# The four token-side sums of the block products: issued inside the first gate chunk, and their transposes spread over the first up chunk

## The chip, the cores and the metric

The kernel runs on one core of a Trainium2 chip. The metric is the device time of one execution in microseconds (us); a kernel is timed in several runs, and the median counts. One execution of each kernel is also profiled: its trace holds every instruction of TensorE (PE, its weight loads apart as PEld), VectorE (DVE), ScalarE (ACT), GpSimd (POOL) and SyncE (SP, which issues most of the transfers), all in us from the start of the span.

## The reference

The program is a two-layer encoder trunk over 256 tokens of width 2048. Each layer has a projection into two groups of heads (attention and retention), an output projection with a residual LayerNorm, and a SwiGLU feed-forward part with another. The change touches the feed-forward part alone:

```
for l in range(DEPTH):                       # DEPTH = 2
    ...                                      # heads, w_out
    x = layer_norm(ALPHA * x + mix, ln1_g[l], ln1_b[l])
    f = (jax.nn.silu(x @ w_gate[l]) * (x @ w_up[l])) @ w_down[l]
    x = layer_norm(ALPHA * x + f, ln2_g[l], ln2_b[l])
```

Here `w_gate` and `w_up` are 2048 x 5632 and `w_down` is 5632 x 2048, all in fp32.

## The kernel before, in words

**Precision by splitting.** Each fp32 operand is split in two parts: `hi`, a rounded copy made by ACT, and `lo`, the rest, made by DVE (`split`, the lines 248 and 249). A product is then three matmuls: hi with hi, hi with lo, lo with hi (`mm_x`, the lines 236 to 238). Weights come in units of at most 128 x 2048 elements (four blocks of 128 rows by 512 columns). Unit by unit they are loaded into a `raw` buffer, split into `hi` and `lo` (three buffers of each), used and given back; `W.done()` marks a unit as used and issues the split of the unit three further on, and loads ahead of that. The split of unit n+3 writes the buffer of unit n, so ACT's cast waits until PE has used unit n up.

**Feed-forward part.** The 5632 columns go in chunks of 512. In each layer chunk 0 is computed plainly (`plain_group`): gate chunk, 4 units; two SiLU evaluations; up chunk, 4 units. The two groups of 128 tokens have a PSUM bank each (`gb0`, `gb1` for the gate, `ub0`, `ub1` for the up chunk). A unit is 12 matmuls of 512 columns for each of the two. The other ten chunks are computed as block products with seven multiplications in place of eight (`strassen_group`). These need four sums of the 128 x 512 quarters of `x`, which don't depend on the chunk: `s_forms` makes them once a layer, in `plain_group`. It issues four sums on DVE (the lines 745 to 748, tiles `sf`), turns each by four transposes on PE into a bank (line 752, tile `pts`, 16 transposes of 128 x 128 in all), and splits each turned sum (tiles `sfh`, `sfl`). The first sum is first used in the third unit of chunk 1.

**What surrounds it.** `x` reaches the gate chunk through the LayerNorm of the attention part. `chunk_head` computes the gate chunk while the norm is still being applied: eight pieces (`norm.apply`: two DVE instructions in place on `res`, the lines 275 and 276, four transposes into a bank `ptx`, a split into `xTh` and `xTl`) are taken off the list `pend` by `pop` between the units. It holds three units at a time, uses them for the first 128 tokens, then for the others, and ends with the fourth unit. By the end of `pop(8)` all eight pieces have been issued, so `res` is final from there on.

**What sets the order.** The code is issued through a tile framework whose scheduler places each instruction in the queue of its engine, mostly in the order of the code. Every engine then works through its queue strictly in that order; an instruction that waits for a semaphore holds up what stands behind it on the engine.

Of the kernel before, what the change touches and what calls it, by code (L numbers as in the profile page):

```python
# [18 lines left out]
P = 128  # L19
# [91 lines left out]
def trunk(ctx: ExitStack, tc: tile.TileContext, x, pos, w, lnp, cols, eye, consts, out):  # L111
    nc = tc.nc
    V, A, PE, G = nc.vector, nc.scalar, nc.tensor, nc.gpsimd
# [8 lines left out]
    xTh = const.tile([P, KD, S], F32R, name="xTh")  # L122
    xTl = const.tile([P, KD, S], F32R, name="xTl")
# [7 lines left out]
    ident = const.tile([P, P], F32, name="ident")  # L131

    def bank(tag_name):
        return psp.tile([P, 512], F32, tag="ps", name=tag_name)
# [96 lines left out]
    def mm_x(ps, ncol, tok, unit, xh, xl, k0, nk, first, last):  # L231
        wh, wl = unit
        for k in range(nk):
            sh = xh[:, k0 + k, tok * P:(tok + 1) * P]
            sl = xl[:, k0 + k, tok * P:(tok + 1) * P]
            PE.matmul(ps[:, :ncol], sh, wh[:, k, :ncol], start=first and k == 0, stop=False)  # L236
            PE.matmul(ps[:, :ncol], sh, wl[:, k, :ncol], start=False, stop=False)  # L237
            PE.matmul(ps[:, :ncol], sl, wh[:, k, :ncol], start=False, stop=last and k == nk - 1)  # L238
# [8 lines left out]
    def split(hi, lo, src):  # L247
        A.copy(hi, src)  # L248
        V.tensor_tensor(lo, src, hi.bitcast(F32), ALU.subtract)  # L249
# [36 lines left out]
    def pop(n=1):  # L286
        for _ in range(n):
            if pend:
                pend.pop(0)()

    def chunk_plain(banks, ncol, nu, xh, xl, k0, first=True, last=True):
        for u in range(nu):
            (unit,) = W.get()
            for tok in range(2):
                mm_x(banks[tok], ncol, tok, unit, xh, xl, k0 + 4 * u, 4, first and u == 0, last and u == nu - 1)
            W.done()

    def chunk_head(banks, ncol, nu, xh, xl):
        units = W.get(3)
        for u in range(3):  # L300
            mm_x(banks[0], ncol, 0, units[u], xh, xl, 4 * u, 4, u == 0, False)
            pop(1)
        pop(1)
        for u in range(3):
            mm_x(banks[1], ncol, 1, units[u], xh, xl, 4 * u, 4, u == 0, False)
            W.done()
            pop(1)
        pop(8)
        for u in range(3, nu):
            (unit,) = W.get()  # L310
            for tok in range(2):
                mm_x(banks[tok], ncol, tok, unit, xh, xl, 4 * u, 4, False, u == nu - 1)
            W.done()
# [55 lines left out]
    first = W.start()  # L369
# [45 lines left out]
    for l in range(DEPTH):  # L415
# [9 lines left out]

        cq = [bank(f"cq{t}") for t in range(2)]
        chunk_head(cq, 512, 4, xTh, xTl)
        if l == 0:
            rope_tables()
        ckv = [bank(f"ckv{t}") for t in range(2)]  # L430
        chunk_plain(ckv, 320, 4, xTh, xTl, 0)

        cqTh = att.tile([P, 4, S], F32R, tag="s1", name="cqTh")
# [117 lines left out]
        for t in range(2):  # L551
            pt = bank("pqr")
# [162 lines left out]
        mixh, mixl = Mix(mixAh, mixRh), Mix(mixAl, mixRl)  # L715
        wb = [bank(f"wo2{t}") for t in range(2)]
        chunk_plain(wb, 512, 4, mixh, mixl, 0)
        for t in range(2):
            resid(wb, 2, t, norm)
# [19 lines left out]
        def vt512(name):  # L739
            return ffp.tile([P, 512], F32, tag="v", bufs=8, name=name)  # L740

        def s_forms():
            x_ = lambda t, c: res[:, t, 512 * c:512 * (c + 1)]
            s1, s2, s3, s4 = (vt512(f"sf{i}") for i in range(4))
            V.tensor_tensor(s1, x_(1, 0), x_(1, 1), ALU.subtract)
            V.tensor_tensor(s2, x_(0, 0), s1, ALU.subtract)
            V.tensor_tensor(s3, x_(1, 0), x_(0, 0), ALU.subtract)
            V.tensor_tensor(s4, x_(0, 1), s2, ALU.subtract)
            for i, t in enumerate((s1, s2, s3, s4)):
                pt = bank("pts")  # L750
                for j in range(4):
                    PE.transpose(pt[:, j * P:(j + 1) * P], t[:, j * P:(j + 1) * P], ident)
                split(sfh[:, i, :, :], sfl[:, i, :, :], pt.rearrange("p (j t) -> p j t", j=4))

        hprev = []
# [10 lines left out]

        def plain_group(c, flush):
            gb = [bank(f"gb{t}") for t in range(2)]
            chunk_head(gb, 512, 4, xTh, xTl)
            sg = []  # L770
            for t in range(2):
                s_ = vt512("sg")
                A.activation(s_, gb[t], AF.Silu)
                sg.append(s_)
            flush()
            s_forms()
            ub = [bank(f"ub{t}") for t in range(2)]
            chunk_plain(ub, 512, 4, xTh, xTl, 0)
            for t in range(2):
                V.tensor_tensor(sg[t], sg[t], ub[t], ALU.mult)  # L780
                hprev.append((t, c, sg[t]))
# [79 lines left out]
        for f0, f1 in FF_PARTS:  # L861
# [4 lines left out]
            for c in range(f0, f1):  # L866
                (strassen_group if c else plain_group)(c, flush)
            first, final = f0 == 0, f1 == NFF
            if final:
                g, b = ln_params(ffp, ("sfh", "sfl"), 2 + 2 * l)  # L870
            nu = f1 - f0
            for n in range(4):
# [11 lines left out]
                else:  # L884
                    last = l == DEPTH - 1
# [114 lines left out]
```

## Time and profile before

| | before |
|---|---|
| runs | 2242.03, 2242.4 and 2243.55 us, median 2242.4 us |
| profiled execution | 2244.02 us; its span, first to last instruction, 2242.2 us |
| PE busy | 2200.6 us, 98% of the span |
| DVE busy | 1591.3 us, 71% |
| ACT busy | 1026.0 us, 46% |
| POOL busy | 35.5 us, 2% |
| moved by DMA | 441.22 MB, 197 GB/s on the mean |
| mean granted TensorE clock | 0.995 of full speed |

Busy is the time in which an engine has at least one instruction under way. Matmuls overlap: one of 512 columns lasts some 0.40 us in the trace, but in an undisturbed stream one begins every 0.233 us. [...]

### The profile page before, as it was taken

How to read it: one execution, taken by the hardware profiler on the slowest of the kernel's cores; microseconds unless marked ns; L12 is line 12 of the kernel's file. 1: busy time of each engine (PE TensorE's matmuls, PEld its weight loads, DVE VectorE, ACT ScalarE, POOL GpSimd, SP SyncE). 2: the span in 40 equal slices, each digit the busy share in tenths (PEclk: the TensorE clock that was granted, in tenths of full speed). 3: DMA queues.
4: the chain of work that ended last, by engine and by line, in shares of the span. 5: the costliest groups of instructions: out<-in, count | busy, mean ns of one | idle time of the engine just before them, and what ended most of it. 6: DMA issues, size and time to landing. Idle time of an engine off the chain costs nothing. (4 is left out here: it accounts for less than half of the span.)

```text
span 2242.2 us, 26855 instructions
## 1 busy us (share of the span) xinstructions
PE 2200.6 (98%) x11084; PEld 1846.4 (82%) x11084; DVE 1591.3 (71%) x1687; ACT 1026.0 (46%) x1089; POOL 35.5 (2%) x46
## 2 busy tenths in 40 slices
PE   7999999899999999999999999999999999999998
PEld 5988988688888888888889899877888888888886
DVE  7565665787688578788675656766866885877976
ACT  3554333454455355455344533334544553544552
POOL 0000000000000000000000000000000000000000
PEclk9999999999999999999999999999999999999999
DMA  7544554566567556475555344545565764666653
GB/s 255 208 150 151 172 204 169 207 199 233 169 208 256 194 204 228 166 255 187 196 196 180 140 170 169 205 171 188 199 247 173 245 225 171 204 244 206 207 206 113
DMA packets 63467, 441.22 MB, mean 197 GB/s; under 512 B 7408, under 2 KB 7664, under 8 KB 11504
## 3 DMA queue, kind: packets, MB, share of 16 engines
q1 hardware_dynamic: 60048, 418.46, 51.2%
q0 software_dynamic: 2880, 20.97, 5.1%
q8 instruction: 87, 1.43, 0.3%
q14 instruction: 36, 0.29, 0.0%
q10 hardware_dynamic: 416, 0.07, 0.0%
HBM read 437.38 MB, written 2.10 MB: 196 GB/s over the span
## 5 line engine op out<-in xcount | busy, mean ns | idle before, releaser
L249 DVE TENSOR_TENSOR lo<-raw,hi 128x1024 fp32r<-128x1024 f32 (+3 forms) x754 | 1033.9, 1407 | 449.5 <-ACT hi L248 447.4
L248 ACT CAST hi<-raw 128x1024 fp32r<-128x1024 f32 (+3 forms) x754 | 875.2, 1199 | 1016.3 <-PE db L238 298.5
L236 PE MATMUL db<-hi,hTh 128*128 128x512 f32 x704 | 277.3, 394 | 0.0
L237 PE MATMUL db<-lo,hTh 128*128 128x512 f32 x704 | 276.8, 393 | 0.0
L238 PE MATMUL db<-hi,hTl 128*128 128x512 f32 x704 | 272.1, 390 | 0.0
L236 PEld LDWEIGHTS db<-hi,hTh 128*128 128x128 f32 x704 | 132.2, 188 | 32.7 <-ACT hTh L248 3.7
L238 PEld LDWEIGHTS db<-hi,hTl 128*128 128x128 f32 x704 | 132.2, 188 | 29.1
L237 PEld LDWEIGHTS db<-lo,hTh 128*128 128x128 f32 x704 | 132.4, 188 | 26.9
L243 PE MATMUL prq<-xTh,hi 128*128 128x256 f32 x512 | 144.7, 283 | 0.0
L244 PE MATMUL prq<-xTl,hi 128*128 128x256 f32 x512 | 143.1, 279 | 0.0
L245 PE MATMUL prq<-xTh,lo 128*128 128x256 f32 x512 | 142.6, 279 | 0.0
L185 DVE TENSOR_TENSOR raw<-raw,raw 128x2048 f32<-128x2048 f32 x60 | 137.2, 2286 | 0.5
L795 PE MATMUL sX<-hi,xTl 128*128 128x512 f32 x320 | 126.6, 395 | 0.0
L794 PE MATMUL sX<-lo,xTh 128*128 128x512 f32 x320 | 126.5, 395 | 0.0
L793 PE MATMUL sX<-hi,xTh 128*128 128x512 f32 x320 | 126.5, 395 | 0.0
L244 PEld LDWEIGHTS prq<-xTl,hi 128*128 128x128 f32 x512 | 96.3, 188 | 0.1
L243 PEld LDWEIGHTS prq<-xTh,hi 128*128 128x128 f32 x512 | 96.2, 188 | 0.1
L245 PEld LDWEIGHTS prq<-xTh,lo 128*128 128x128 f32 x512 | 96.2, 188 | 0.0
L795 PE MATMUL sQ<-hi,xTl 128*128 128x512 f32 x240 | 94.9, 395 | 0.0
L794 PE MATMUL sQ<-lo,xTh 128*128 128x512 f32 x240 | 94.9, 395 | 0.0
L793 PE MATMUL sQ<-hi,xTh 128*128 128x512 f32 x240 | 94.9, 395 | 0.0
L685 DVE SCALAR_TENSOR_TENSOR res<-res,db 128x512 f32<-128x512 f32 x64 | 43.8, 685 | 67.8 <-PE db L238 67.8
(265 smaller groups left out, 3998.2 us busy)
## 6 DMA issues: line engine op xcount, KB each, us to landing
raw<-w SPq DMA_DIRECT2D x377, 1024.0 KB, 4.9
raw<-w POOLq DMA_DIRECT2D x20, 1024.0 KB, 8.4
raw<-w SPq DMA_DIRECT2D x8, 640.0 KB, 3.8
lng<-lnp SPq DMA_DIRECT2D x4, 1024.0 KB, 4.8
lnb<-lnp SPq DMA_DIRECT2D x4, 1024.0 KB, 5.6
res<-x SPq DMA_DIRECT2D x4, 512.0 KB, 6.4
out<-res SPq DMA_DIRECT2D x8, 256.0 KB, 2.6
cst<-consts SPq DMA_DIRECT2D x2, 976.5 KB, 8.1
```

The costliest lines, as they stand in the source:

```text
L185: V.tensor_tensor(r[into], r[into], r[frm], ALU.add)
L236: PE.matmul(ps[:, :ncol], sh, wh[:, k, :ncol], start=first and k == 0, stop=False)
L237: PE.matmul(ps[:, :ncol], sh, wl[:, k, :ncol], start=False, stop=False)
L238: PE.matmul(ps[:, :ncol], sl, wh[:, k, :ncol], start=False, stop=last and k == nk - 1)
L243: PE.matmul(ps_ap, wh[:, k, c0:c0 + P], xh[:, k, :], start=k == 0, stop=False)
L244: PE.matmul(ps_ap, wh[:, k, c0:c0 + P], xl[:, k, :], start=False, stop=False)
L245: PE.matmul(ps_ap, wl[:, k, c0:c0 + P], xh[:, k, :], start=False, stop=k == nk - 1)
L248: A.copy(hi, src)
L249: V.tensor_tensor(lo, src, hi.bitcast(F32), ALU.subtract)
L793: PE.matmul(ps, a, wh[:, k, :], start=first and k == 0, stop=False, skip_group_check=True)
L794: PE.matmul(ps, a, wl[:, k, :], start=False, stop=False, skip_group_check=True)
L795: PE.matmul(ps, b, wh[:, k, :], start=False, stop=k == 3, skip_group_check=True)
```

## The change

The four sums are issued by `s_sums`, which `chunk_head` calls behind `pop(8)`, ahead of the fourth unit of the gate chunk. The transposes and splits of the turned sums are issued by `s_turn(u)`, which `chunk_plain` calls ahead of unit u of the up chunk: none ahead of unit 0, two sums ahead of unit 1, one ahead of unit 2, one ahead of unit 3. The number of instructions stays the same: per layer 4 sums, 16 transposes, 4 casts, 4 subtractions. `chunk_plain` and `chunk_head` act as before where they are called without `then`.

```diff
-    def chunk_plain(banks, ncol, nu, xh, xl, k0, first=True, last=True):
+    def chunk_plain(banks, ncol, nu, xh, xl, k0, first=True, last=True, then=None):
         for u in range(nu):
+            if then is not None:
+                then(u)
             (unit,) = W.get()
...
-    def chunk_head(banks, ncol, nu, xh, xl):
+    def chunk_head(banks, ncol, nu, xh, xl, then=None):
...
         pop(8)
+        if then is not None:
+            then()
         for u in range(3, nu):
...
-        def s_forms():
+        sforms = []
+
+        def s_sums():
             x_ = lambda t, c: res[:, t, 512 * c:512 * (c + 1)]
-            s1, s2, s3, s4 = (vt512(f"sf{i}") for i in range(4))
+            sforms.extend(vt512(f"sf{i}") for i in range(4))
+            s1, s2, s3, s4 = sforms
...
-            for i, t in enumerate((s1, s2, s3, s4)):
+
+        def s_turn(u):
+            for i in ((), (0, 1), (2,), (3,))[u]:
                 pt = bank("pts")
                 for j in range(4):
-                    PE.transpose(pt[:, j * P:(j + 1) * P], t[:, j * P:(j + 1) * P], ident)
+                    PE.transpose(pt[:, j * P:(j + 1) * P], sforms[i][:, j * P:(j + 1) * P], ident)
                 split(sfh[:, i, :, :], sfl[:, i, :, :], pt.rearrange("p (j t) -> p j t", j=4))
...
-            chunk_head(gb, 512, 4, xTh, xTl)
+            chunk_head(gb, 512, 4, xTh, xTl, s_sums)
...
             flush()
-            s_forms()
             ub = [bank(f"ub{t}") for t in range(2)]
-            chunk_plain(ub, 512, 4, xTh, xTl, 0)
+            chunk_plain(ub, 512, 4, xTh, xTl, 0, then=s_turn)
```

What this makes of the queues is shown for layer 0; layer 1 has the same rows with other numbers. A row is an instruction with its line, the tiles written and read, and in brackets the semaphores that it waits for.

On PE, before: the end of the gate chunk, all transposes of the sums, and the start of the up chunk (`hi65` and `lo65` are the two parts of its first unit, which the counting of all weights numbers 65).

```order
L238 MATMUL gb1_3513<-hi64_3598,xTl_72 128x512
L752 MATMUL pts_3708<-ident_79,sf0_3700 128x128 [waits DMAHW3_49,DMAHW2_49,DMAHW5_49,DMAHW1_49,DMAHW6_49,DMAHW0_49,DMAHW7_49,DVE_49,PE_49]
L752 MATMUL pts_3708<-ident_79,sf0_3700 128x128 x3
L752 MATMUL pts_3715<-ident_79,sf1_3701 128x128 [waits DVE_49,PE_49]
...
L236 MATMUL ub0_3736<-hi65_3627,xTh_71 128x512 [waits PE_49]
```

On PE, of the change: the same place, and the two further places at which transposes now stand ahead of a unit (the first two sums ahead of unit 66, the third ahead of unit 67; the fourth stands likewise ahead of unit 68).

```order
L238 MATMUL gb1_3513<-hi64_3598,xTl_72 128x512
L236 MATMUL ub0_3708<-hi65_3627,xTh_71 128x512 [waits PE_49]
...
L236 MATMUL ub1_3709<-hi65_3627,xTh_71 128x512 [waits PE_49]
...
L761 MATMUL pts_3742<-ident_79,sf0_3664 128x128 [waits DMAHW3_49,DMAHW5_49,DMAHW2_49,DMAHW6_49,DMAHW1_49,DMAHW7_49,DMAHW0_49,PE_49]
...
L761 MATMUL pts_3749<-ident_79,sf1_3665 128x128 [waits PE_49]
...
L236 MATMUL ub0_3708<-hi66_3656,xTh_71 128x512 [waits Activation_49]
...
L761 MATMUL pts_3786<-ident_79,sf2_3666 128x128 [waits PE_49]
```

The up chunk now follows the gate chunk directly. Its first matmul of either bank waits for PE's own count alone, and the first transposes no longer wait for DVE by themselves (the unit before them already did, for later work of DVE).

On DVE, before: the last norm pieces (`res`), the `lo` parts of the weight units 64 to 67 with the last two splits of `x` between them, and then the sums.

```order
L276 SCALAR_TENSOR_TENSOR res_70<-res_70,rs_3497,lnb1_3062 128x512 [waits DVE_49] x2
L249 TENSOR_TENSOR lo64_3599<-raw64_3431,hi64_3598 128x1024 [waits DMAHW2_49,Activation_49]
...
L249 TENSOR_TENSOR xTl_72<-ptx_3608,xTh_71 128x4x128 [waits Activation_49]
...
L249 TENSOR_TENSOR lo67_3689<-raw67_3604,hi67_3688 128x1024 [waits DMAHW7_49,Activation_49]
L249 TENSOR_TENSOR lo67_3689<-raw67_3604,hi67_3688 128x1024 [waits Activation_49]
L745 TENSOR_TENSOR sf0_3700<-res_70 128x512
L746 TENSOR_TENSOR sf1_3701<-res_70,sf0_3700 128x512 [waits DVE_49]
L747 TENSOR_TENSOR sf2_3702<-res_70 128x512
L748 TENSOR_TENSOR sf3_3703<-res_70,sf1_3701 128x512 [waits DVE_49]
```

On DVE, of the change: the same stretch.

```order
L276 SCALAR_TENSOR_TENSOR res_70<-res_70,rs_3497,lnb1_3062 128x512 [waits DVE_49] x2
L752 TENSOR_TENSOR sf0_3664<-res_70 128x512 [waits DVE_49]
L753 TENSOR_TENSOR sf1_3665<-res_70,sf0_3664 128x512 [waits DVE_49]
L754 TENSOR_TENSOR sf2_3666<-res_70 128x512
L249 TENSOR_TENSOR lo64_3599<-raw64_3431,hi64_3598 128x1024 [waits DMAHW2_49,Activation_49]
...
L249 TENSOR_TENSOR xTl_72<-ptx_3637,xTh_71 128x4x128 [waits Activation_49]
L755 TENSOR_TENSOR sf3_3667<-res_70,sf1_3665 128x512 [waits DVE_49]
L249 TENSOR_TENSOR lo66_3657<-raw66_3489,hi66_3656 128x1024 [waits DMAHW4_49,Activation_49]
```

Three sums now stand right behind the last norm pieces, ahead of the `lo` part of unit 64, and the fourth ahead of that of unit 66. Two or three matmuls at the start of the gate chunk's fourth unit also change places with their neighbours on PE.

## Rows read from the trace of the kernel before

**Rows 1.** Page, part 1: busy us, share of the span and instructions of each engine.

```profile
PE 2200.6 (98%) x11084; PEld 1846.4 (82%) x11084; DVE 1591.3 (71%) x1687; ACT 1026.0 (46%) x1089; POOL 35.5 (2%) x46
```

**Rows 2.** Timeline of PE, layer 0: start, us, line, tiles, [idle before <- releaser].

```profile
416.67 0.43 PE L238 MATMUL gb<-hi,xTl 128*128 128x512 f32 x1
...
424.18 0.40 PE L238 MATMUL gb<-hi,xTl 128*128 128x512 f32 x1
428.76 3.32 PE L752 MATMUL pts<-ident,sf 128*128 128x128 f32 x16 [4.18 <-issue]
...
433.66 0.40 PE L238 MATMUL ub<-hi,xTl 128*128 128x512 f32 x1
...
453.73 0.40 PE L237 MATMUL ub<-lo,xTh 128*128 128x512 f32 x1
```

**Rows 3.** Timeline of PE, layer 1, from the end of the gate chunk.

```profile
1529.46 0.40 PE L238 MATMUL gb<-hi,xTl 128*128 128x512 f32 x1
1534.04 3.65 PE L752 MATMUL pts<-ident,sf 128*128 128x128 f32 x16 [4.18 <-issue]
...
1539.42 0.39 PE L238 MATMUL ub<-hi,xTl 128*128 128x512 f32 x1
```

**Rows 4.** Timeline of DVE, layer 0, second half of the gate chunk.

```profile
410.32 1.41 DVE L276 SCALAR_TENSOR_TENSOR res<-res,rs,lnb 128x512 f32<-128x512 f32 x2
413.59 2.36 DVE L249 TENSOR_TENSOR lo<-raw,hi 128x1024 fp32r<-128x1024 f32 x2 [1.86 <-ACT hi L248]
415.87 0.68 DVE L249 TENSOR_TENSOR xTl<-ptx,xTh 128x512 fp32r<-128x512 f32 x1
...
425.69 2.36 DVE L249 TENSOR_TENSOR lo<-raw,hi 128x1024 fp32r<-128x1024 f32 x2 [3.00 <-ACT hi L248]
427.97 0.69 DVE L745 TENSOR_TENSOR sf<-res 128x512 f32<-128x512 f32 x1
...
429.90 0.68 DVE L748 TENSOR_TENSOR sf<-res,sf 128x512 f32<-128x512 f32 x1
```

**Rows 5.** Timeline of ACT, layer 0, end of the gate chunk and start of the up chunk.

```profile
424.62 1.99 ACT L248 CAST hi<-raw 128x1024 fp32r<-128x1024 f32 x2 [1.46 <-PE gb L238]
426.51 0.59 ACT L773 ACTIVATE sg<-gb 128x512 f32<-128x512 f32 x1
...
438.30 2.00 ACT L248 CAST hi<-raw 128x1024 fp32r<-128x1024 f32 x2 [5.60 <-PE ub L238]
```

**Rows 6.** Chain that ended last, layer 1: start, length, what; single steps and transposes within streams.

```profile
1529.87 4.17 issue
1534.04 3.65 PE pts L752 x16
1537.68 0.43 PE ub L236
...
1539.35 0.23 PE ub L237
...
1569.21 0.87 PE pth L762 x8
```

**Rows 7.** Chain of layer 1's gate chunk: four transposes within a stream.

```profile
1520.99 0.44 PE ptx L280 x4
```

**Rows 8.** Windows: us, busy us of PE, PEld, DVE, ACT, POOL, granted clock, DMA share, GB/s.

```profile
395.00:424.40 29.40, 27.70 (x126) 20.91 (x124) 24.80 (x33) 13.79 (x18) 0.93 (x1) 1.00 0.68 253
424.40:434.00 9.60, 5.28 (x24) 4.34 (x24) 7.44 (x10) 4.83 (x7) 0.00 (x0) 0.82 0.75 288
434.00:454.00 20.00, 20.00 (x88) 16.09 (x87) 9.91 (x7) 5.91 (x5) 1.04 (x1) 1.00 0.24 73
1529.70:1540.00 10.30, 6.12 (x25) 5.43 (x25) 7.54 (x10) 4.83 (x7) 0.00 (x0) 0.67 0.84 321
```

**Rows 9.** Timeline of SP, layer 0: issue of the load of unit 68.

```profile
419.21 0.33 SPq L147 DMA_DIRECT2D raw<-w  x1
```

**Rows 10.** Line 147 from 411 to 445 us: eight loads of 1 MB, time to landing.

```profile
DMA to landing us min/median/max: 4.6/5.3/8.1
```

## Prediction, made before the changed kernel was run

> **What bounds the kernel now.** I read the page first: PE is busy for 98% of the span, every other engine far less [rows 1], so time can be won only where PE stands still, runs slowly, or does work that need not be there. Then the chain that ended last. Around the first chunk of the feed-forward part it is PE nearly throughout, with one break that stands out in layer 1: 4.17 us of "issue", 3.65 us of the sums' transposes, and then up-chunk matmuls at 0.43 us each before they are back at 0.23 [rows 6]. Then the timelines of the place, engine by engine, in both layers; the numbers that follow are layer 0 unless layer 1 is named.
>
> On PE the last gate matmul starts at 424.18 and the first transpose at 428.76, after 4.18 us idle [rows 2]; layer 1 has the same 4.18 [rows 3]. The profile names no releaser ("issue"), so the cause is read from the other engines. The first sum runs on DVE from 427.97 for 0.69 us and ends at 428.66, 0.10 us before the first transpose. Ahead of it DVE waited 3.00 us for ACT and then made the `lo` part of unit 67 [rows 4]. ACT made the `hi` part from 424.62, having waited for the last gate matmul [rows 5], since it writes the buffer which the gate chunk's last unit frees. So the stall is a loop: PE finishes the gate chunk, ACT may cast unit 67, DVE may subtract, only then come the sums that stand behind it in DVE's queue, and only then may PE go on. The sums' own input was final at 411.73, when the last norm pieces ended (410.32 + 1.41) [rows 4], some 16 us earlier. What waits on PE behind the transposes, the up chunk, needs none of them.
>
> The stop has a second price. Over the 9.6 us from the end of the gate chunk the granted clock is 0.82 on the mean, against 1.00 before and after; in layer 1 it is 0.67 [rows 8]. PE idled, the clock went to its half level, and transposes and the first up matmuls ran slowly.
>
> **The change part by part.**
>
> *The stop goes.* An undisturbed matmul starts every 0.233 us: 86 starts lie between the sixth and the 92nd of the up chunk, 433.66 and 453.73, 20.07 / 86 [rows 2]. From the last gate matmul to the sixth up matmul six steps should take 1.40 us. Before, they take 433.66 - 424.18 = 9.48, so 8.08 us are lost in layer 0 [rows 2]; in layer 1 1539.42 - 1529.46 = 9.96, so 8.56 [rows 3]. Together 16.64 us: idle time, 16 transposes a layer, slow clock. In the new queue the up chunk follows the gate chunk directly; its first unit's split and both banks are ready (its first matmuls wait for PE's own count only, as the rows of the change show). I count all 16.64 as removed.
>
> *The transposes come back inside the stream.* The trace has the like: eight transposes between block-product matmuls take 0.87 us of the chain [rows 6], four in the gate chunk 0.44 [rows 7]. The change has one group of eight and two of four: 0.87 + 2 x 0.44 = 1.75 us a layer, 3.50 in all. They wait for nothing new: by the first of them (24 up matmuls after 424.41, near 430.0) the sums are long done. Bounds: nothing at best if part of a group hides under weight loads, and 3.65 a layer if they ran as slowly as before [rows 6]. I take 1.75, since both rows are the same operation in the same kind of stream.
>
> *The sums move ahead on DVE.* Three of them follow the last norm piece, where DVE idled 1.86 us. From the first sum's start to the fourth's lie 1.93 us for three, so from 411.73 they end at 413.66 where the `lo` part of unit 64 began at 413.59 [rows 4]: 0.07 us late. Behind it is the second-last split of `x`, which ends at 416.55 [rows 4], and whose first reader on PE starts at 416.67 [rows 2]. That margin of 0.12 covers it, and the scheduler has moved further matmuls ahead of that reader. The fourth sum falls in front of unit 66's `lo` part, whose use is some 9 us later. Cost taken: nothing; if the cover were missing, at most the 1.93 us a layer.
>
> *Casts and subtractions of the turned sums move into the up chunk.* Four casts (0.6 us each) and four subtractions (0.69) now stand between the splits of weight units. In 20 us of the up chunk DVE is busy 9.91 us and ACT 5.91 [rows 8], so 2.8 and 2.4 us more fit. Nearest to late would be unit 68: its load is issued at 419.21 [rows 9] and at the longest landing time, 8.1 us [rows 10], is there by 427.3; its cast begins when the first up unit is used up, now near 430.2 in place of 438.30 [rows 5], and with 2 us for the cast and half a `lo` more it is split by 433.6. It is used at about 442.5. The turned sums are first needed in chunk 1. Cost: nothing.
>
> *Transfers.* The loads ahead of the up chunk hang on DVE's `lo` parts of units 65 to 67, whose times hardly change; in the up chunk DMA had a share of 0.24 [rows 8]. Work after it simply moves forward.
>
> **The sum.** 16.64 - 3.50 = 13.14 us. The profiled execution took 2244.02 us, its span 2242.2; less 13.14 that is 2230.9 and a span of 2229.1. The median of the runs shown, 2242.4, lies 1.6 below the profiled execution, so the forecast is 2242.4 - 13.1 = 2229.3 us, 0.59% faster. A change of 0.2%, 4.5 us, is about what a measurement of this kernel can tell from none.
>
> **The rivals.**
>
> *A new, smaller wait takes the stop's place.* Had the up chunk's first bank been one that a SiLU must empty, PE would stand until the second SiLU ends at 427.10 (426.51 + 0.59) [rows 5], 2.7 us a layer: 2234.7. The rows of the change speak against it. Had the sums no cover on DVE, 1.93 a layer: 2233.2. Middle of these cases and the forecast: about 2232.
>
> *The transposes stay slow.* With the clock at its half level they cost 3.65 a layer in place of 1.75: 2229.3 + 3.8 = 2233.1. Against it stand eight in 0.87 us within a stream, 0.11 each, where the slow ones took 3.65 / 16 = 0.23 [rows 6]. [...]
>
> *The change doesn't remove the wait.* The profile names no releaser, and the first transposes wait for seven DMA counts as well as for DVE. Were one of these the cause, and met only after some work that has moved too, the 4.35 us a layer from 424.18 + 0.23 to 428.76 would come back ahead of unit 66 with its slow clock: 2238 to 2242. Against it: the transposes began 0.10 us after the first sum ended.
>
> *The clock falls in the up chunk.* This is the case on the other side. If breaks for transposes pulled the clock to half there, a matmul would cost 0.43 in place of 0.233 [rows 6], 0.197 more; over the 2 x 96 of both up chunks 37.8 us, 2267. It turns into a loss once more than 13.1 / 0.197 = 67 of the 192 ran slowly. Against it: groups of transposes stand in the gate chunk as well, and its clock is 1.00 throughout [rows 8].
>
> **How the numbers follow.** Forecast 0.78, with an own range of 2227.5 to 2231 from the spread of the runs (1.5 us) and the price of the transposes; new smaller wait 0.13; slow transposes 0.02; wait not removed 0.04; clock falls 0.03. The first three are faster by over 0.2%: 0.93; the fourth is within: 0.04; the last is slower: 0.03. The range that holds 8 in 10 reaches from 2227 to 2233.5, so to the lesser waits of the first rival.
>
> **What the changed profile would show.** In both layers no idle PE before the first `ub` matmul, which starts 0.23 to 0.3 us after the last `gb` one; granted clock 1.00 from the gate chunk through the up chunk; the sums on DVE at 411.7, the `lo` part of unit 64 within 0.1 us of 413.6; groups of eight, four and four transposes at 0.87, 0.44 and 0.44 us; the up chunk's last matmul 6.3 us earlier in layer 0 and 13.1 earlier in layer 1, and PE busy time lower by some 5 us (13.14 less twice the 4.18 of idle). I would be wrong if PE waited ahead of a unit of the up chunk or ahead of chunk 1, if a `gb` matmul came to wait for the split of `x`, or if the shorter pause let a later stage wait for its weights.

## The result, and the profile of the changed kernel

The changed kernel runs in 2230.9 us (median of four runs, 2230.61 to 2231.03), the kernel before in 2242.98 us on the same chip (four runs, 2242.03 to 2244.04): a ratio of 0.9946, 95% interval 0.9929 to 0.9963. It is faster by 12.1 us on the medians and by 13.0 us on the profiled executions (spans of 2242.2 and 2229.2 us; the prediction gave 2229.1).

The page, part 1, answers to [rows 1]:

```profile
PE 2196.6 (99%) x11084; PEld 1844.2 (83%) x11084; DVE 1590.2 (71%) x1687; ACT 1025.2 (46%) x1089; POOL 35.5 (2%) x46
```

PE has the same number of instructions and is busy 4.0 us less. The two stops of 4.18 us in [rows 2] and [rows 3] are gone, 8.4 of the 13.0 us that the span lost; nearly all the rest is the transposes and the first up-chunk matmuls behind them, which now take less time (before, 4.90 us in layer 0 and 5.38 us in layer 1 from the first transpose to the start of the sixth of these matmuls).

The timeline of PE at the place in layer 0, against [rows 2]:

```profile
424.37 0.40 PE L238 MATMUL gb<-hi,xTl 128*128 128x512 f32 x1
424.60 0.40 PE L236 MATMUL ub<-hi,xTh 128*128 128x512 f32 x1
...
429.97 0.39 PE L238 MATMUL ub<-hi,xTl 128*128 128x512 f32 x1
430.20 1.04 PE L761 MATMUL pts<-ident,sf 128*128 128x128 f32 x8
430.99 0.48 PE L236 MATMUL ub<-hi,xTh 128*128 128x512 f32 x1
431.30 0.39 PE L237 MATMUL ub<-lo,xTh 128*128 128x512 f32 x1
...
436.43 0.39 PE L238 MATMUL ub<-hi,xTl 128*128 128x512 f32 x1
436.66 0.60 PE L761 MATMUL pts<-ident,sf 128*128 128x128 f32 x4
437.01 0.48 PE L236 MATMUL ub<-hi,xTh 128*128 128x512 f32 x1
437.33 0.39 PE L237 MATMUL ub<-lo,xTh 128*128 128x512 f32 x1
...
448.73 0.40 PE L801 MATMUL sX<-hi,xTh 128*128 128x512 f32 x1
```

No row has idle time in brackets. The first up-chunk matmul starts 0.23 us after the last gate matmul; before, the first transpose started 4.58 us after it and the first up-chunk matmul, at 431.73, 7.55 us after it. The price of the eight transposes is read from starts: from 429.97 to 430.99 the stream takes 1.02 us where one step takes 0.23, so 0.79, and the step behind them is 0.31 instead of 0.23: together 0.87. In the same way four of them cost 437.01 - 436.43 - 0.23 = 0.35, and the step behind them is 0.09 longer than usual: 0.44. The first matmul of chunk 1 (`sX`) starts at 448.73, before at 454.90.

The timeline of DVE in the gate chunk, against [rows 4]:

```profile
410.57 1.40 DVE L276 SCALAR_TENSOR_TENSOR res<-res,rs,lnb 128x512 f32<-128x512 f32 x2
412.00 0.69 DVE L752 TENSOR_TENSOR sf<-res 128x512 f32<-128x512 f32 x1
412.73 0.69 DVE L753 TENSOR_TENSOR sf<-res,sf 128x512 f32<-128x512 f32 x1
413.34 0.68 DVE L754 TENSOR_TENSOR sf<-res 128x512 f32<-128x512 f32 x1
413.94 2.35 DVE L249 TENSOR_TENSOR lo<-raw,hi 128x1024 fp32r<-128x1024 f32 x2
...
419.93 0.68 DVE L755 TENSOR_TENSOR sf<-res,sf 128x512 f32<-128x512 f32 x1
...
431.48 2.36 DVE L249 TENSOR_TENSOR lo<-raw,hi 128x1024 fp32r<-128x1024 f32 x2 [3.23 <-ACT hi L248]
```

The 1.86 us in which DVE idled ahead of the `lo` part at 413.59 are filled by three sums. That `lo` part now starts at 413.94; the whole execution runs 0.25 us later at this point (the norm piece above started at 410.32 before), so the sums push it by 0.10 us.

The timeline of ACT around the up chunk, against [rows 5]:

```profile
424.80 2.00 ACT L248 CAST hi<-raw 128x1024 fp32r<-128x1024 f32 x2 [0.99 <-PE gb L238]
426.70 0.59 ACT L782 ACTIVATE sg<-gb 128x512 f32<-128x512 f32 x1
430.40 2.00 ACT L248 CAST hi<-raw 128x1024 fp32r<-128x1024 f32 x2 [3.11 <-PE ub L238]
432.30 1.07 ACT L248 CAST sfh<-pts 128x512 fp32r<-128x512 f32 x2
```

The cast of unit 68 starts at 430.40 and its `lo` part on DVE is done at 433.84 (431.48 + 2.36); the casts of the turned sums fit behind it.

The windows from the end of the gate chunk to the start of chunk 1, in layer 0 and layer 1, against [rows 8] (busy us of PE, PEld, DVE, ACT, POOL, then granted clock, DMA share, GB/s):

```profile
424.40:447.60 23.20, 23.20 (x110) 18.90 (x109) 14.56 (x13) 10.33 (x12) 1.04 (x1) 1.00 0.55 191
1523.30:1546.60 23.30, 23.30 (x110) 18.97 (x109) 14.56 (x13) 10.33 (x12) 0.91 (x1) 1.00 0.54 188
```

PE is busy all the time at a granted clock of 1.00; before it was 0.82 and 0.67 over the first ten microseconds. In the chain that ended last, layer 1 has one step of 0.87 us for the first eight transposes, where [rows 6] had 4.17 us of "issue" and 3.65 us for all sixteen:

```profile
1528.95 0.23 PE ub L238
1529.18 0.87 PE pts L761 x8
1530.05 0.23 PE ub L236
```

### The profile page after: what moved, and what is told of

Read it like the earlier page. It is cut to its first block, busy times and chain, and to the rows that moved or that the text cites. A ratio compares the mean times of both kernels' runs of the same rounds, so it can differ in the third digit from the quotient of the medians.

```text
span 2229.2 us, 26848 instructions
## 1 busy us (share of the span) xinstructions
PE 2196.6 (99%) x11084; PEld 1844.2 (83%) x11084; DVE 1590.2 (71%) x1687; ACT 1025.2 (46%) x1089; POOL 35.5 (2%) x46
```

## The experiments

**Each half of the change alone.** The change moves the sums ahead and the transposes back. My theory, a loop of waits through DVE's queue, says that either half breaks it. The first kernel keeps the early sums and turns all four ahead of the up chunk:

```diff
-            for i in ((), (0, 1), (2,), (3,))[u]:
+            for i in ((0, 1, 2, 3), (), (), ())[u]:
```

> Of the change only its first half: the sums are issued within the gate chunk, all 16 transposes of a layer stand together ahead of the up chunk, where they stood before. My theory, that the stop was the sums' place in the DVE queue behind the split that waits for the gate chunk's last matmul: no idle PE ahead of the transposes, clock 1.00, 16 transposes in about 1.5 to 1.75 us, so as fast as the whole change, 12 to 13 us under the kernel before (2230 to 2231.5 us where before takes 2243). Rival, that spreading the transposes is what counts (banks, casts or the place itself): a stop of over 2 us a layer stays, 2235 us or more.

Measured: 2230.96 us (five runs, 2230.0 to 2231.23), ratio to before 0.9944 (0.993 to 0.9957). The second leaves the sums where they were and spreads the transposes:

```diff
-            chunk_head(gb, 512, 4, xTh, xTl, s_sums)
+            chunk_head(gb, 512, 4, xTh, xTl)
...
             flush()
+            s_sums()
```

> Of the change only its second half: the sums stay behind the gate chunk (and behind the split of unit 67 on DVE), the transposes are spread ahead of the up units 1, 2 and 3. My theory: the sums are done by about 430.6 us, the first two by 429.4, and the first transposes are due at 430.2, so PE doesn't wait for them either and the up chunk's first unit fills the time: 2230.5 to 2231.5 us, as the whole change. Rival, that the sums must be early: the first transposes wait ahead of unit 66, by 1 us or more a layer, 2233 us or more.

Measured: 2231.12 us (2229.95 to 2231.39), ratio 0.9943 (0.993 to 0.9955). So either half is sufficient by itself, and the two together gain no more than one. The timeline of PE in the kernel with early sums shows sixteen transposes in one go, right behind the gate chunk:

```profile
423.33 0.39 PE L238 MATMUL gb<-hi,xTl 128*128 128x512 f32 x1
423.56 1.91 PE L761 MATMUL pts<-ident,sf 128*128 128x128 f32 x16
425.23 0.48 PE L236 MATMUL ub<-hi,xTh 128*128 128x512 f32 x1
425.54 0.39 PE L237 MATMUL ub<-lo,xTh 128*128 128x512 f32 x1
```

They take 425.23 - 423.56 = 1.67 us and 0.08 in the step behind, 1.75 in all, the same as in three groups. The row is 1.91 us long; the row of the same sixteen transposes had 3.32 us in [rows 2] and 3.65 us in [rows 3]. In the other kernel the margin is thin, as rows of its DVE timeline and of its PE timeline show:

```profile
428.26 0.69 DVE L752 TENSOR_TENSOR sf<-res 128x512 f32<-128x512 f32 x1
428.98 0.69 DVE L753 TENSOR_TENSOR sf<-res,sf 128x512 f32<-128x512 f32 x1
```

```profile
430.30 1.03 PE L761 MATMUL pts<-ident,sf 128*128 128x128 f32 x8
```

The second sum is there at 429.67, and its transposes belong to the group that starts at 430.30. In this kernel the sums ended that late at no cost: PE had the first unit of the up chunk ahead of their transposes, from 424.70 on.

**The slow clock by itself.** How much of the 16.64 us was the clock? Filling the pause of the kernel before with 36 unneeded matmuls of 256 columns leaves the loop of waits as it is and keeps PE at work:

```diff
             V.tensor_tensor(s4, x_(0, 1), s2, ALU.subtract)
+            pf = bank("pfill")
+            for i in range(36):
+                PE.matmul(pf[:, :256], xTh[:, i % KD, :P], xTh[:, i % KD, :], start=True, stop=True)
```

> The kernel before, with 36 matmuls of 256 columns of x with itself ahead of the sums' transposes, into a bank that nobody reads; at 0.117 us each they fill the 4.2 us in which PE stood still. My theory, that of the 16.6 us some 8.7 are idle time and the rest is the low clock after it: transposes and first up matmuls run at full clock, the transposes now paced by the sums (one per 0.6 us, the fourth done at 430.6), so the up chunk starts near 431.0 in place of 431.73 in layer 0 and near 1536.3 in place of 1537.34 in layer 1, and no up matmul is slow: 3.4 us faster than before in all, about 2239.6 us where before takes 2243. Rival, that the transposes and the first up matmuls were slow for another reason (casts, banks, semaphores): no gain, 2243 us.

Measured: 2241.05 us (11 runs, 2240.52 to 2242.63), ratio to before 0.9989 (0.998 to 0.9998), 2.65 us under the 2243.7 of the kernel before on this chip. The timeline of PE and a window of the place:

```profile
424.93 0.40 PE L238 MATMUL gb<-hi,xTl 128*128 128x512 f32 x1
425.16 4.48 PE L751 MATMUL pfill<-xTh 128*128 128x256 f32 x36
429.50 2.60 PE L755 MATMUL pts<-ident,sf 128*128 128x128 f32 x16
431.86 0.48 PE L236 MATMUL ub<-hi,xTh 128*128 128x512 f32 x1
...
433.11 0.40 PE L238 MATMUL ub<-hi,xTl 128*128 128x512 f32 x1
```

```profile
424.40:434.00 9.60, 9.45 (x65) 8.29 (x65) 7.25 (x10) 4.83 (x7) 0.00 (x0) 1.00 0.82 329
```

The granted clock is 1.00 now. From the last gate matmul to the sixth of the up chunk it takes 433.11 - 424.93 = 8.18 us, where [rows 2] have 9.48: 1.30 us gained in layer 0, and 1.77 in layer 1 (8.19 against the 9.96 of [rows 3]). So the low clock accounts for 3.07 of the 16.64 us (3.4 were expected); the other 13.57 are the wait and the transposes at a granted clock of 1.00. PE being busy did not help otherwise: this kernel shows 9.45 of 9.60 us busy and is 10 us slower than the changed one.

**What the transposes cost.** If the sums cost PE 3.50 us, a kernel without them must be faster by that much. The first try lets the block products use quarters of `x` in place of the sums:

```diff
-            chunk_head(gb, 512, 4, xTh, xTl, s_sums)
+            chunk_head(gb, 512, 4, xTh, xTl)
...
-            chunk_plain(ub, 512, 4, xTh, xTl, 0, then=s_turn)
+            chunk_plain(ub, 512, 4, xTh, xTl, 0)
...
-            s1, s2, s3, s4 = ((sfh[:, i], sfl[:, i]) for i in range(4))
+            s1, s2, s3, s4 = ((xTh[:, 4 * i:4 * i + 4, 0:P], xTl[:, 4 * i:4 * i + 4, 0:P]) for i in range(4))
```

> The changed kernel without sums, transposes and their splits; the block products take quarters of x in their place, so part of the computation is left out. My theory, that 16 transposes cost 1.75 us a layer inside the stream and nothing else of the four sums is on the path: 3.5 us less than the change, about 2227.4 us, and PE's gate and up chunks otherwise the same. Rival, that the transposes hide under weight loads: 2230.9 us. Rival, that sums and splits still hold PE up somewhere: under 2226.5 us.

Measured: 2231.14 us (2230.43 to 2231.68), no gain at all. The expectation missed by 3.7 us, and PE's timeline shows where (first `sX` matmul of chunk 1 and one late in layer 0):

```profile
447.13 0.40 PE L799 MATMUL sX<-hi,xTh 128*128 128x512 f32 x1
...
1009.33 0.40 PE L799 MATMUL sX<-hi,xTh 128*128 128x512 f32 x1
```

In the changed kernel the same two start at 448.73 and 1009.34. The 1.60 us are there at the start of chunk 1 and are lost again, little by little, over the block products. What differs there is the tile that stands in PE as weights: `x` where the sums were. (The two tiles of the sums are gone as well, which can move tiles allocated behind them.) So the second try keeps the tiles of the sums and fills them with copies of quarters of `x`, without sums and transposes:

```diff
-                pt = bank("pts")
-                for j in range(4):
-                    PE.transpose(pt[:, j * P:(j + 1) * P], sforms[i][:, j * P:(j + 1) * P], ident)
-                split(sfh[:, i, :, :], sfl[:, i, :, :], pt.rearrange("p (j t) -> p j t", j=4))
+                src = xTh[:, 4 * i:4 * i + 4, 0:P].bitcast(F32)
+                A.copy(sfh[:, i, :, :], src)
+                V.tensor_tensor(sfl[:, i, :, :], src, sfh[:, i, :, :].bitcast(F32), ALU.subtract)
```

> The kernel without sums and transposes, once more: now the tiles sfh and sfl are filled with copies of quarters of x (the same four casts and four subtractions a layer, at the same places), so the block products read the tiles that they read in the change; the sums are left out of the computation. The kernel that read x itself lost in the block products what it won in the up chunks: its matmuls with x as weights started every 0.2333 us, those with the sums' tiles as weights every 0.229 to 0.230. If that was the tile and not the transposes, and 16 transposes cost 1.75 us a layer as I said: 3.5 us less than the change, 2227.4 us, span about 2225.7. Rival, that the transposes cost nothing or that the values make the difference: 2230.5 to 2231 us.

Measured: 2227.2 us (2226.74 to 2227.86), ratio 0.9926 (0.9914 to 0.9939), 3.7 us under the changed kernel; its span of 2225.4 us is 3.8 shorter. Against the kernel before, measured beside it, it gains 16.3 us, where the changed kernel gained 12.1. Its timeline has the two `sX` matmuls at

```profile
447.11 0.40 PE L789 MATMUL sX<-hi,xTh 128*128 128x512 f32 x1
...
1007.68 0.40 PE L789 MATMUL sX<-hi,xTh 128*128 128x512 f32 x1
```

1.62 and 1.66 us ahead of the changed kernel, and nothing is lost between them. The transposes' price of 3.50 us holds to within some 0.7 us. The values are not what makes the difference: the low parts are zero here (a rounded copy less itself), yet the 960 matmuls with the sums' tiles take 221.8 us in all, summed from each start to PE's next, against 221.9 in the changed kernel. And a second thing has come up: the same number of matmuls of the same form takes a different time with another tile: from the first of these two `sX` matmuls to the second 562.20 us with `x` itself, 560.57 with the copies and 560.61 in the changed kernel.

**Where the tiles lie.** The last five kernels change no instruction's kind or number, only the width or the place of a small constant tile of the norms, `mhalf`, and so the addresses of the tiles behind it. By the layout of the compiled program, which no view of the profile shows, `x` of the changed kernel lies 32 bytes (modulo 256) behind the high halves of the weights, the sums 192. Widening `mhalf` by 32 bytes puts all weights and sums up by that, and `x` at a distance of 0:

```diff
-    mhalf = const.tile([P, 8], F32, name="mhalf")
+    mhalf = const.tile([P, 16], F32, name="mhalf")
```

> The changed kernel with one small tile made 64 bytes wide in place of 32, which moves every tile behind it by 32 bytes: the weights (hi, lo), the sums and h then start at a multiple of 64 bytes as x does, the attention output at 32 beyond one. Before, weights, sums and h all lay at 32 beyond a multiple of 64, x and the attention output at a multiple; matmuls of sums and h with weights started every 0.228 to 0.231 us, of x and the attention output every 0.233 to 0.234. If a matmul is faster where both operands lie alike: the some 3400 matmuls with x gain 4 ns each, about 14 us, 2217 us. If it is faster where its stationary operand lies at 32: the 3000 with sums and h lose 4 ns each, the 770 of the attention output gain, 2240 us. If it is the values: 2230.9 us. If an unaligned moving operand is what costs: all matmuls gain, well under 2210 us.

Measured: 2216.55 us (2216.39 to 2216.61), ratio 0.9878 (0.9865 to 0.9892), 14.3 us under the changed kernel. The counter-test allocates `mhalf` at its old width ahead of `x`, so that `x` alone moves by 32 bytes:

```diff
+    mhalf = const.tile([P, 8], F32, name="mhalf")
...
-    mhalf = const.tile([P, 8], F32, name="mhalf")
```

> The changed kernel with the same small tile, at its old width, allocated ahead of x: only x moves by 32 bytes, so x, weights, sums and h all lie at 32 beyond a multiple of 64. If a matmul is faster where both operands lie alike, or where the stationary one lies at 32: the some 3400 matmuls with x as weights gain 4 ns each, about 14 us, 2217 us. If it is the values: 2230.9 us. If only an aligned moving operand helps: 2230.9 us as well.

Measured: 2232.02 us (2231.45 to 2232.81). It missed: in this version neither a place alike modulo 64 bytes nor a stationary operand at 32 beyond a multiple of 64 brought a gain. Three more widths, 24, 32 and 48 columns, were to tell whether the distance modulo 256 is:

> The changed kernel with mhalf at 24 columns in place of 8: all tiles behind it move 64 bytes up, so the first address of x stands 224 bytes (modulo 256) behind that of the high halves of the weights it is multiplied with. In the runs so far the spacing of 512-column matmuls went with that distance: 0 gave 0.227 us, 192 gave 0.229, 32, 64 and 96 gave 0.2332 to 0.234. Theory 'the distance modulo 256 sets the spacing': a value of its own for x at 224, between 0.227 and 0.2334, so between 2216 and 2231 us, and if it goes with how far the distance lies below 256, close to 0.228 and 2217. Rival 'only equal places are fast': 0.233, 2231. Rival 'not the distance, something else in the layout': no relation.

Measured: 2232.66 us (2232.39 to 2233.22), no gain, and above the range that the theory gave.

> The changed kernel with mhalf at 32 columns: the tiles behind it move 96 bytes, x stands 192 bytes (modulo 256) behind the high halves, as the sums and the up chunks' activations do in every kernel so far, whose matmuls start 0.229 us apart. Theory 'the distance modulo 256 sets the spacing': x at 0.229 as well, a gain of about two thirds of that of the version with 16 columns (2216.55), so about 2220 us. Rival 'only equal places are fast': 0.233, 2231 us.

Measured: 2209.47 us (two runs, 2208.49 and 2210.46), ratio to before 0.9848 (0.9819 to 0.9877): the fastest of all, 10.5 us under what was expected.

> The changed kernel with mhalf at 48 columns: the tiles behind it move 160 bytes, x stands 128 bytes (modulo 256) behind the high halves, half way round. No kernel so far had 128. Theory 'the distance modulo 256 sets the spacing': between the 0.229 of 192 and the 0.234 of 96, so 2220 to 2232 us. Rival 'only equal places are fast': 0.233, 2231 us.

Measured: 2232.85 us (2232.65 to 2233.37), no gain. With 48 columns the weights lie at a multiple of 64 bytes again, as they do with 16, so an aligned streaming operand, the theory that the counter-test had left, wasn't enough for a gain in this kernel either. What was measured in these five stands in the last section.

## Why the prediction was right

**The stop goes (16.64 us).** Right in kind and size. The loop of waits was inferred from other engines, since the profile named no releaser; the two halves, each enough to break it (2230.96 and 2231.12 us), show it. So do the starts of the first sum on DVE: 412.00 in the changed kernel, where it is queued ahead of unit 64's `lo` part, but 427.97 in the kernel before and 428.26 in the second half alone, where the same sum is queued behind unit 67's. The filled version takes the sum apart. The wait from the last gate matmul to the first transpose, less one step, is 4.35 us a layer, 8.70 together. The transposes' own work is 3.50. The low clock is 3.07. The remaining 1.4 us come from PE following the sums one by one: in the filled version sixteen transposes take 2.36 us a layer against 1.67 without that wait. One reading of the working holds in layer 1 alone, by windows of the kernel before: there the granted clock was at 0.50 by the end of the pause (1533.00 to 1534.04) and over the transposes (1534.04 to 1537.69). In layer 0 it stayed at 1.00 through the pause and the first microsecond of the transposes (424.50 to 429.80) and was 0.51 only from 429.80 to 433.15.

**The transposes come back (3.50 us).** Right: 0.87, 0.44 and 0.44 us a layer in the trace, and 3.7 us by the runs without them. They did not stay slow: the row of sixteen was 1.91 us long behind a stream, at a granted clock of 1.00; it was 3.65 us long behind the pause of layer 1, at 0.50, and 2.60 us in the filled version, at 1.00 but at the pace of the sums. The instructions are the same in all three; what differed was when the sums came, what PE did ahead of the transposes and, between the pause and the other two, the granted clock.

**Sums, casts, transfers (nothing).** Right, with the covers that were named: the idle DVE ahead of unit 64 (0.10 us late, 0.07 was worked out), and unit 68 split by 433.84 (433.6 was said, though its own terms, 430.2 with 2 for the cast and 1.2 for half a `lo`, add up to 433.4) for a use at about 443. Neither of the lesser waits of the first rival came up, and PE waits nowhere in either up chunk.

**The sum.** The first matmul of chunk 1, before in both layers and then after in layer 1:

```profile
454.90 0.40 PE L793 MATMUL sX<-hi,xTh 128*128 128x512 f32 x1
...
1560.65 0.40 PE L793 MATMUL sX<-hi,xTh 128*128 128x512 f32 x1
```

```profile
1547.55 0.40 PE L801 MATMUL sX<-hi,xTh 128*128 128x512 f32 x1
```

In layer 0 chunk 1 starts at 448.73 against 454.90, 6.17 us earlier, or 6.36 counted from the last gate matmul (424.37 against 424.18); 6.3 was said. In layer 1 it starts at 1547.55 against 1560.65, 13.10 us earlier; 13.1 was said. The span fell by 13.0 us for 13.14 forecast.

**The one size that was off** is the last step, from the profiled execution to the median: I carried the 1.6 us, by which the median of before lay below its profiled run, over to the changed kernel. Its runs lie within some 0.4 us of one another and its median 0.1 below its profiled run, so 2230.9 came out in place of 2229.3, just inside the forecast's own range, which ended at 2231. The runs of before spread over 2.0 us, and their median of three was a draw from that, on the low side: the 31 further runs of that kernel, in three sets, have medians of 2243.1 to 2243.7. And PE's busy time fell by 4.0 us where 5 were said: subtracting the idle time from the sum gives 4.78. Of the 0.8 between, 0.6 lie in the first 40 us of the program, far ahead of the change, where PE was busy 23.79 us in place of 23.19.

## What to carry to other kernels

A long idle row of PE without a named releaser is read from the other engines' queues: find the last instruction that ended just ahead of it, and ask what it was queued behind rather than what it needed. Here 2 us of DVE work with its input ready 16 us before stood behind a buffer that PE itself had to free; to move either the work ahead of that buffer's instruction or its reader on PE behind the next stream was enough (2230.96 and 2231.12 us against 2243.7), and the slow clock behind the pause, 3.07 us, went with it: the granted clock of that place was 1.00 in both versions, 0.82 before. Price such a change from starts in an undisturbed stream, and against profiled executions on both sides, not against a median on one.

## What the runs showed of the hardware that was not expected

The spacing of this kernel's 512-column matmuls with `x` fell from 0.2335 us to 0.2270 and 0.2287 in two of the five versions that move tiles. Read from the first 24 up-chunk matmuls, start of the first to start of the last over 23 steps, the changed kernel takes (429.97 - 424.60) / 23 = 0.2335 us a step. The timelines of the versions with `mhalf` at 16 and at 32 columns, in this order:

```profile
426.39 0.39 PE L236 MATMUL ub<-hi,xTh 128*128 128x512 f32 x1
...
431.61 0.40 PE L238 MATMUL ub<-hi,xTl 128*128 128x512 f32 x1
```

```profile
419.78 0.39 PE L236 MATMUL ub<-hi,xTh 128*128 128x512 f32 x1
...
425.04 0.39 PE L238 MATMUL ub<-hi,xTl 128*128 128x512 f32 x1
```

That is 0.2270 us with `x` at a distance of 0, and 0.2287 at 192, the distance at which the sums lie in the changed kernel. All at the same granted clock of 1.00. By the same reading `x` at 64, 128 and 224 gave 0.2330, 0.2322 and 0.2335, and those versions ran in 2232.02, 2232.85 and 2232.66 us, no gain. Why the version at 192 is nonetheless the fastest is seen in the matmuls of 256 columns of the projections, where the roles are swapped and `x` streams. The first and the last of 270 rows of `prq` in layer 0, for the changed kernel, for 16 and for 32 columns:

```profile
205.07 0.37 PE L243 MATMUL prq<-xTh,hi 128*128 128x256 f32 x1
...
236.84 0.28 PE L245 MATMUL prq<-xTh,lo 128*128 128x256 f32 x1
```

```profile
205.48 0.36 PE L243 MATMUL prq<-xTh,hi 128*128 128x256 f32 x1
...
237.84 0.28 PE L245 MATMUL prq<-xTh,lo 128*128 128x256 f32 x1
```

```profile
202.40 0.37 PE L243 MATMUL prq<-xTh,hi 128*128 128x256 f32 x1
...
232.99 0.28 PE L245 MATMUL prq<-xTh,lo 128*128 128x256 f32 x1
```

31.77, 32.36 and 30.59 us for the same rows: of these three, what was best for the long matmuls (0) was worst for the short ones, and 192 was faster than the changed kernel in both. Over the whole kernel, summed from each start to PE's next, the 3600 matmuls of 512 columns with `x` take 858.6, 838.3 and 843.5 us in the three versions, and the 2304 of 256 columns 272.2, 278.4 and 265.2. That makes 14.1 and 22.1 us less than in the changed kernel, where the spans are 14.4 and 22.6 us shorter. The matmuls in which `x` streams were no part of the distance theory as it stood; their 7.0 us (272.2 less 265.2) are most of the 10.5 by which its 2220 us was too high.

What is shown: the placement alone moved this kernel between 2209 and 2233 us, nearly twice as much as the change under study, and two placements beat it. In these runs the time also went with the two places relative to one another, not with the address of each alone: in the four widened versions weights, sums and `h` all move together, by 32 to 160 bytes, and their matmuls kept their time (summed from start to start, those with `h` 485.5 to 485.7 us in all, those with the sums 221.0 to 221.9), while those with `x`, which stays, changed in two of the four (838.3 and 843.5 us against 858.6). What stays open is the rule. The distance modulo 256 is consistent with every version tried, but each distance of `x` was seen in one version only, its values follow no order that I can name (0 and 192 fast; 32, 64, 128 and 224 not), no run tests 256, which I assumed, against another period, and no run shows the cause. For a prediction the lesson is smaller: the spacing of an "undisturbed" stream went here with the layout, and a wider tile ahead of the operands changed it in two of the four widened versions (0.2270 and 0.2287 us in place of 0.2335). The change under study did not: its block products took 560.61 us between the two `sX` matmuls (448.73 and 1009.34), and 560.63 before (454.90 and 1015.53).
